# Modulation columns of an MLA layer: twelve more units on TensorE column groups, the last gate's rows moved to the output projection

## The chip, the cores and the metric

The kernel runs on one core of one Trainium2 chip. The metric is device time in microseconds (us) of one execution. Engines are written PE (TensorE), DVE (VectorE), ACT (ScalarE), POOL (GpSimd) and SP (SyncE, whose queue issues the transfers from HBM).

## The reference, cut to what matters

The program computes two blocks, one behind the other, in fp32, on a sequence of 512 tokens and a context of 256, with a width D of 1024. Everything that the change touches lies in the first layer of the first block, an attention layer with low-rank projections (MLA), and in the modulation of that layer and the next:

```python
def modulation(cond, w, bias):
    m = jax.nn.silu(cond) @ w + bias
    return jnp.split(m, 3, axis=-1)

def first_block(x, c, ctx, c_ctx, ada_w, ada_b, norm_g, ...):
    for i in range(DEPTH):                       # DEPTH = 2
        sx, scx, gx = (m[:, None, :] for m in modulation(c, ada_w[i], ada_b[i]))
        sc, scc, gc = modulation(c_ctx, ada_w[i], ada_b[i])
        hx = rms_norm(x, norm_g[i]) * (1 + scx) + sx
        hc = rms_norm(ctx, norm_g[i]) * (1 + scc) + sc
        ...                                      # mixer: h @ w_in, attention, @ w_out
        x = x + gx * yx
        if i < DEPTH - 1:
            ctx = ctx + gc * yc
```

So per layer the vectors `silu(c)` and `silu(c_ctx)` are multiplied with a 1024 x 3072 matrix `ada_w[i]`: shift, scale and gate. The gate of the first layer is needed for both conditions at its output projection, shift and scale of the second layer right behind it, and the gate of the second layer only for `c`, later still.

## The kernel before, in words

Activations lie with the width on the 128 partitions, in eight tiles `k` of 128, and the 768 tokens (256 of context, then 512) along the free dimension. A matrix product in fp32 is made of three PE passes over halves (`mm3`, lines 534 to 538): weights and activations are each split into a rounded high half and the rest (`wh`, `wl`, `hh`, `hl`), and PE multiplies `hh` with `wh`, `hl` with `wh` and `hh` with `wl`. For weights, `wsplit` (from line 511) lets ACT make `wh` (line 519) and DVE make `wl` (line 520); the buffers hold three units, so a unit's split waits until PE has read the unit three before it. `Stream` loads two units by one transfer of 1 MB.

`mla` has three stages. **The input projection** has 14 units of 128 columns. Units 0 to 2 run side by side, over k: for each k, `modulated` (lines 678 to 688) makes `hh` and `hl` from the normed input, with `xr` as the step between (line 686), and then all three units take that k. Units 3 to 13 run one after the other, each over all k, 48 matmuls a unit; ACT evicts units 0 to 4 into `cq`, and units 6 to 13 through Silu into `gate`.

The shift and scale of the first layer come from `modulation(k)`, eight units of 256 columns. Each takes 1 MB of `ada0`, makes eight matmuls of 32 columns (line 776; `sc` holds both conditions in its first columns) that stand in four column groups of the array, copies the result to `mrow` on ACT, sums the four groups and turns the row into columns by two matmuls with the selector `sel` (line 781), and DVE puts them into `md0`. Three places of the tile `ada0` take the loads in turn.

All other modulation columns, 32 tiles of 128, come from `ada_rows`, called after each unit of the projection: 512 KB of the transposed table `adat` go into one of five places, in the still unused ends of `gate` and `cq`, and per row tile and condition one instruction multiplies it with `silu(c)`, spread over all partitions in `crow`, and sums along the free dimension into one column of `mcol`. Most of it is on DVE (line 715). For the second condition two of three row tiles are multiplied on POOL (line 711) and summed on ACT (line 700).

**The attention** of 16 heads stands between, and **the output projection** (`project`, from line 893) has eight units: per unit 24 matmuls for the context and 24 for the sequence, the eviction `L900` on DVE, which multiplies with the gate column of `mcol` and adds to `xc` or `x`, the square on ACT (line 905) and its sum on DVE. The last three units run their context parts first.

The order of each engine's queue is set by a scheduler that goes by the order of the program, with some work lifted ahead (`wsplit` and `wraw` by an offset `WOFF`). The queues are in order, that of SP too: a transfer that waits for its place holds up all behind it.

Of the kernel before, what the change touches and what calls it, by code (L numbers as in the profile page):

```python
# [18 lines left out]
P = 128  # L19
# [76 lines left out]
def layout(inp):  # L96
# [9 lines left out]
    a["crow"] = np.concatenate([f["c"].reshape(1, D), f["c_ctx"].reshape(1, D)], 0)  # L106
# [3 lines left out]
    a["ada0"] = _units(u, KT, 2 * P)  # L110
    rows = np.concatenate([aw[0][:, 2048:].T, aw[1].T], 0).reshape(32, P, D)
    a["adat"] = rows
# [365 lines left out]
class Kern:  # L478
# [211 lines left out]
    def ada_load(self, i):  # L690
        if i < 32:
            self.dma(self.ada_ring[i % len(self.ada_ring)], self.ins["adat"][i])

    def ada_rows(self, n):

        for _ in range(n):
            i = self.ada_i
            if self.ada_pending:
                junk, acc = self.ada_pending.pop()
                self.S.activation(junk, junk, AF.Copy, accum_out=acc)  # L700
            if i >= 32:
                return
            self.ada_i += 1
            w = self.ada_ring[i % len(self.ada_ring)]
            for cond in range(2):
                if cond == 1 and i >= 24:
                    continue
                acc = self.mcol[:, cond, i:i + 1]
                if cond and i % 3:
                    junk = self.apool.tile([P, D], F32, tag="sq", name="junk", bufs=3)  # L710
                    self.G.tensor_tensor(junk, w, self.crow[:, cond], op=ALU.mult)
                    self.ada_pending.append((junk, acc))
                else:
                    junk = self.apool.tile([P, D], BF16, tag="jb", name="junk", bufs=1)
                    self.V.scalar_tensor_tensor(junk, w, 1.0, self.crow[:, cond], op0=ALU.mult, op1=ALU.mult,
                                                accum_out=acc)
            self.ada_load(i + len(self.ada_ring))

    def mla(self):
# [3 lines left out]
        self.ada_i, self.ada_pending = 0, []  # L723
        with ExitStack() as mst:
# [10 lines left out]
            with ExitStack() as st:  # L735
                A = self.apool = self.pool("mlaA", stack=st)
                xt = A.tile([P, KT, TA], F32, tag="xt", name="xt")
                self.crow = A.tile([P, 2, D], F32, name="crow")
# [6 lines left out]
                row = ada0[0:1, 2]  # L745
                self.dma(row, ins["crow"])
# [4 lines left out]
                for k in range(2):  # L751
                    self.dma(ada0[:, k], ins["ada0"][k])
                G.memset(sc, 0.0)
                S.activation(row, row, AF.Silu)
# [4 lines left out]
                for cond in range(2):  # L759
                    G.partition_broadcast(self.crow[:, cond], row[:, cond * D:(cond + 1) * D], channels=P)  # L760
# [3 lines left out]
                def modulation(k):  # L764

                    if k >= KT:
                        return
                    if k >= 2:
                        self.dma(ada0[:, k % 3], ins["ada0"][k])
                    raw = ada0[:, k % 3].rearrange("p (k f) -> p k f", f=2 * P)  # L770
                    md = self.md0[:, k]
# [11 lines left out]
                    V.tensor_scalar(md[:, 0], pm[:, :2], self.vcol("ada_b", k), None, op0=ALU.add)  # L783
                    V.tensor_scalar(md[:, 1], pm[:, 2:], ab1[:, k:k + 1], self.vcol("norm_g", k), op0=ALU.add, op1=ALU.mult)

                acc = self.sumsq(A, [xt[:, k] for k in range(KT)], TA, eng=V, bufs=3)
                self.norm_acc(A, R, acc, TA, D, bufs=3)
                modulation(0)
                win = self.wstream(ins["mw_in"], 14, 2, P)
                fps = [[self.b1(), self.b1()] for _ in range(3)]  # L790
                first = [next(win) for _ in fps]
                modulation(1)
                for k in range(KT):
                    md = self.md0[:, k]
                    self.modulated(A, hh[:, k], hl[:, k], xt[:, k], R, (md[:, 1, 1:2], md[:, 1, 0:1]),
                                   (md[:, 0, 1:2], md[:, 0, 0:1]), segs, "sq", 3)
                    modulation(k + 2)
                    for w, pt in zip(first, fps):
                        for (o, n), ps in zip(segs, pt):
                            self.mm3(ps[:, :n], (w[0][:, k], w[1][:, k]), (hh[:, k, o:o + n], hl[:, k, o:o + n]),  # L800
                                     k == 0, k == KT - 1)
                self.dma(rope, ins["rope"])
                self.woff = WOFF
                cq = A.tile([P, KT, TA], F32, tag="xt", name="cq")
                self.ada_ring = [z[:, o * D:(o + 1) * D] for z, m in (
                    (gate[:, 4:].rearrange("p k t -> p (k t)"), 3), (cq[:, 5:].rearrange("p k t -> p (k t)"), 2))
                    for o in range(m)]
                for i in range(len(self.ada_ring)):
                    self.ada_load(i)
# [896 lines left out]
```

## Time and profile before

| | |
|---|---|
| time of three runs | 1989.47, 1992.1 (median), 1992.36 us |
| profiled execution | 1991.66 us, span of the trace 1989.9 us |
| PE busy | 1874.2 us, 94% of the span |
| DVE busy | 1356.7 us, 68% |
| ACT busy | 948.9 us, 48% |
| POOL busy | 653.9 us, 33% |
| input projection, first to last matmul | 31.4 to 193.4 us of the span |
| output projection, first to last eviction | 499.2 to 557.1 us |

The shares are averages over stages with different limits: PE is busy nearly all the time in most of the program, so what matters for this change is where it is not, in the first 200 us. The times of a row are counted from the start of the span. A busy PE need not be a PE at full clock: the profile lists the granted clock of each stretch.

### The profile page before, as it was taken

The numbers are of one execution on the slowest core, as the hardware profiler recorded it, in microseconds if no ns is written. First come the engines' busy times: TensorE is split into PE (matmuls) and PEld (weight loads), VectorE is DVE, ScalarE is ACT, GpSimd is POOL, SyncE is SP. The second block draws the span as 40 slices with busy tenths as digits, with TensorE's granted clock in tenths as the row PEclk, the third lists the DMA queues.
The fourth block names the chain that finished last, engine by engine and source line by source line (L and its number), as shares of the span: only waits on it lengthen the run. The fifth ranks groups of instructions, "written<-read, shape, count | busy, mean of one in ns | idle before, by whom it ended". The sixth has DMA issues, their size and how long they took to land.

```text
span 1989.9 us, 25452 instructions
## 1 busy us (share of the span) xinstructions
PE 1874.2 (94%) x9842; PEld 1592.4 (80%) x9842; DVE 1356.7 (68%) x1856; ACT 948.9 (48%) x1623; POOL 653.9 (33%) x532
## 2 busy tenths in 40 slices
PE   5888999999989999898889999999999999999997
PEld 3777888898879999787658888888788888888886
DVE  4896777778475556789986666666744466666666
ACT  4463767777264544766535333333422343333333
POOL 0473766755002222555630212121400002121213
PEclk8998999999999999999889999999999999999998
DMA  8543000101121111132112223222222323222221
GB/s 308 184 162 131 27 1 28 43 22 64 53 73 43 44 43 65 49 118 98 48 53 106 106 85 106 88 103 89 96 91 85 106 85 105 86 106 85 106 88 61
DMA packets 33419, 171.28 MB, mean 86 GB/s; under 512 B 3505, under 2 KB 6833, under 8 KB 17809
## 3 DMA queue, kind: packets, MB, share of 16 engines
q1 hardware_dynamic: 33298, 169.65, 24.2%
q8 instruction: 77, 1.26, 0.3%
q14 instruction: 44, 0.36, 0.1%
HBM read 167.54 MB, written 2.10 MB: 85 GB/s over the span
## 4 chain that ended last, share of the span: by engine, by line
PE 46%; DVE 3%; issue 1%; ACT 1%; POOL 0%; DVEq 0%; POOLq 0%; ACTq 0%
PE b L536 15%; PE b L538 15%; PE b L537 15%; DVE cv L1538 0%; DVE x L1657 0%; DVE hl L503 0%; DVE wl L520 0%; DVE hr L1528 0%; DVE x L599 0%; ACT wh L519 0%; PE b L625 0%; DVE yl L499 0%; DVE gt L1275 0%; POOL cv L1569 0%; DVE b L1521 0%
## 5 line engine op out<-in xcount | busy, mean ns | idle before, releaser
L538 PE MATMUL b<-hh,wl 128*128 128x512 f32 (+1 forms) x1248 | 482.8, 388 | 17.1 <-DVE wl L520 17.1
L536 PE MATMUL b<-hh,wh 128*128 128x512 f32 (+1 forms) x1248 | 485.4, 392 | 9.5 <-ACT hh L687 5.1
L537 PE MATMUL b<-hl,wh 128*128 128x512 f32 (+1 forms) x1248 | 482.6, 387 | 3.6 <-DVE hl L503 3.6
L519 ACT CAST wh<-raw 128x1024 fp32r<-128x1024 f32 (+1 forms) x257 | 263.5, 1026 | 462.5 <-PE b L537 416.1
L538 PEld LDWEIGHTS b<-hh,wl 128*128 128x128 f32 x1248 | 239.2, 192 | 68.2 <-DVE wl L520 17.9
L520 POOL TENSOR_TENSOR wl<-raw,wh 128x1024 fp32r<-128x1024 f32 (+1 forms) x68 | 166.2, 2446 | 381.1 <-ACT wh L519 374.4
L520 DVE TENSOR_TENSOR wl<-raw,wh 128x1024 fp32r<-128x1024 f32 (+1 forms) x189 | 246.8, 1308 | 60.6 <-ACT wh L519 56.6
L536 PEld LDWEIGHTS b<-hh,wh 128*128 128x128 f32 x1248 | 238.2, 191 | 58.8 <-ACT hh L687 6.1
L537 PEld LDWEIGHTS b<-hl,wh 128*128 128x128 f32 x1248 | 239.3, 192 | 56.3 <-DVE hl L503 4.9
L1538 DVE SCALAR_TENSOR_TENSOR cv<-u,vec,cv 128x511 f32<-128x511 f32 x192 | 181.0, 943 | 41.3 <-ACT cv L1536 39.3
L1564 DVE TENSOR_TENSOR u<-b,Rp 128x512 f32<-128x512 f32 x88 | 60.8, 691 | 157.5 <-PE b L538 157.0
L1569 POOL TENSOR_TENSOR cv<-cv 128x512 f32<-128x512 f32 x44 | 57.2, 1300 | 267.8 <-DVE cv L1538 211.6
L536 PE MATMUL b<-ah,wh 128*128 128x512 f32 (+1 forms) x368 | 140.1, 382 | 0.0
L538 PE MATMUL b<-ah,wl 128*128 128x512 f32 (+1 forms) x368 | 140.0, 381 | 0.0
L537 PE MATMUL b<-al,wh 128*128 128x512 f32 (+1 forms) x368 | 139.8, 380 | 0.0
L1589 DVE TENSOR_TENSOR x<-x,b 128x512 f32<-128x512 f32 x160 | 105.3, 679 | 11.3 <-PE b L538 11.0
L536 PE MATMUL b<-wh,hh 128*128 128x256 f32 (+1 forms) x320 | 95.7, 301 | 2.6 <-ACT wh L519 2.6
L1536 ACT ACTIVATE cv<-u,vec 128x512 f32<-128x512 f32 x96 | 78.2, 814 | 35.7 <-DVE u L1564 35.7
L537 PE MATMUL b<-wl,hh 128*128 128x256 f32 (+1 forms) x320 | 93.8, 293 | 0.0
L1024 DVE TENSOR_REDUCE st<-b 128x1 f32<-128x768 f32 (+1 forms) x96 | 74.0, 772 | 28.9 <-PE b L538 28.1
L538 PE MATMUL b<-wh,hl 128*128 128x256 f32 (+1 forms) x320 | 93.1, 293 | 0.0
L1029 POOL TENSOR_SCALAR p<-p,st 128x768 f32<-128x768 f32 (+1 forms) x96 | 73.5, 768 | 56.2 <-DVE st L1028 49.5
(399 smaller groups left out, 3997.8 us busy)
## 6 DMA issues: line engine op xcount, KB each, us to landing
raw<-in_fw_up SPq DMA_DIRECT2D x44, 1024.0 KB, 4.8
raw<-in_fw_dn SPq DMA_DIRECT2D x22, 1024.0 KB, 4.8
raw<-in_ow_in SPq DMA_DIRECT2D x12, 1024.0 KB, 4.8
gate<-in_adat SPq DMA_DIRECT2D x20, 512.0 KB, 4.5
ada<-in_ada SPq DMA_DIRECT2D x8, 1024.0 KB, 7.6
raw<-in_mw_in SPq DMA_DIRECT2D x7, 1024.0 KB, 6.3
cq<-in_adat SPq DMA_DIRECT2D x12, 512.0 KB, 3.5
raw<-in_mw_out SPq DMA_DIRECT2D x4, 1024.0 KB, 4.9
```

Of the source, the lines that this page charges most:

```text
L519: self.S.copy(hi, raw[:, o:o + w])
L520: (leng or self.V).tensor_tensor(lo, raw[:, o:o + w], hi.bitcast(F32), op=ALU.subtract)
L536: m(out, w[0], x[0], start=start, stop=False)
L537: m(out, w[0], x[1], start=False, stop=False)
L538: m(out, w[1], x[0], start=False, stop=stop)
L1024: V.tensor_reduce(st[:, 0:1], sv, axis=AX.XY, op=ALU.max, negate=True)
L1029: G.tensor_scalar(p[:, :nk * P], p[:, :nk * P], st[:, 2:3], 0.0, op0=ALU.mult, op1=ALU.add)
L1536: self.S.activation(v, u, AF.Identity, bias=col(3), scale=col(2))
L1538: self.V.scalar_tensor_tensor(v[:, sh:], u[:, :T - sh], col(tap), v[:, sh:], op0=ALU.mult, op1=ALU.add)
L1564: V.tensor_tensor(u, ps, R, op=ALU.mult)
L1569: G.tensor_tensor(cv[0], cv[0], cv[1], op=ALU.mult)
L1589: V.tensor_tensor(self.x[:, 4 * j + f], self.x[:, 4 * j + f], ps, op=ALU.add)
```

## The change

The 24 row tiles that hold the first layer's gate and the second layer's shift and scale are taken from DVE and POOL and become twelve more units of 256 columns, of the kind of `modulation(k)`, which is now split into `ada_load`, `ada` (the load's use: eight matmuls and the copy to `mrow`) and `columns` (the selector matmuls and what DVE makes of them). Units 8 and 9 stand behind units 0 to 2 of the projection, then one stands behind each unit up to the twelfth; the selector matmuls of each come a unit later, ahead of its k = 6. Their loads go into a ring of three places of 1 MB: a tile `spare`, the end of `cq` and the end of `gate`. The eight row tiles of the second layer's gate stay on DVE, for `c` alone, in the output projection (`gate1`), with a buffer `g1` of one place and with `crow` loaded there. At the start of the program the squares of the odd tiles are summed by PE and those of the even ones by DVE. `silu` on one partition and the two broadcasts on POOL go.

```diff
     a["crow"] = f["c"].reshape(1, D)
...
-    def ada_rows(self, n):
-
-        for _ in range(n):
-            i = self.ada_i
-            if self.ada_pending:
-                junk, acc = self.ada_pending.pop()
-                self.S.activation(junk, junk, AF.Copy, accum_out=acc)
...
-                if cond and i % 3:
-                    junk = self.apool.tile([P, D], F32, tag="sq", name="junk", bufs=3)
-                    self.G.tensor_tensor(junk, w, self.crow[:, cond], op=ALU.mult)
-                    self.ada_pending.append((junk, acc))
-                else:
-                    junk = self.apool.tile([P, D], BF16, tag="jb", name="junk", bufs=1)
-                    self.V.scalar_tensor_tensor(junk, w, 1.0, self.crow[:, cond], op0=ALU.mult, op1=ALU.mult,
-                                                accum_out=acc)
-            self.ada_load(i + len(self.ada_ring))
...
+                def ada(i):
+
+                    raw = slots[i].rearrange("p (k f) -> p k f", f=2 * P)
 
                     pr = self.b1()[:, :2 * P]
                     for kk in range(KT):
                         j = 32 * (kk % 4)
                         PE.matmul(pr[j:j + 32], sc[:, kk], raw[:, kk], start=(kk < 4), stop=(kk >= 4))
-                    mrow = A.tile([P, 2 * P], F32, tag="mrow", name="mrow", bufs=1)
+                    mrow = A.tile([P, 2 * P], F32, tag="mrow", name="mrow", bufs=2)
                     S.copy(mrow, pr)
+                    return i, mrow
+
+                def columns(i, mrow):
+
                     pm = self.b1()[:, :4]
                     for part in range(2):
                         PE.matmul(pm[:, 2 * part:2 * part + 2], mrow[:, part * P:(part + 1) * P], sel,
                                   start=True, stop=True)
...
+                    c = 2 * (i - KT)
+                    V.tensor_copy(self.mcol[:, :, c:c + 2], pm.rearrange("p (k c) -> p c k", c=2))
...
-                acc = self.sumsq(A, [xt[:, k] for k in range(KT)], TA, eng=V, bufs=3)
+                for k in range(KT):
+                    q = acc if k == 0 else A.tile([P, TA], F32, tag="sq", name="sq", bufs=3)
+                    i = S.activation(q, xt[:, k], AF.Square)
+                    if k % 2:
+                        for (o, e), ps in zip(segs0, pss):
+                            PE.matmul(ps[:, :e - o], self.ones, q[:, o:e], start=k == 1, stop=False)
+                    elif k:
+                        V.tensor_tensor(acc, acc, q, op=ALU.add)
...
+                ring = [spare, cq[:, 5:].rearrange("p k t -> p (k t)")[:, :2048],
+                        gate[:, 5:].rearrange("p k t -> p (k t)")[:, :2048]]
+                last = 20
+                for i in range(KT, last):
+                    slots[i] = ring[(i - KT) % 3 if i < 19 else 0]
+                for i in range(KT, KT + 3):
+                    ada_load(i)
+                rest = iter(range(KT, last))
+                rows = []
...
                     for k in range(KT if u >= len(fps) else 0):
+                        if k == 6 and rows:
+                            columns(*rows.pop())
                         for (o, n), ps in zip(segs, pt):
...
-                    self.ada_rows(3 if u < 3 else 4)
+                    for i in ((next(rest, None),) if u > 1 else ()):
+                        if i is not None:
+                            rows.append(ada(i))
+                            if i + 3 < 19:
+                                ada_load(i + 3)
...
+                def gate1(f):
+                    w = C.tile([P, D], F32, tag="g1", name="g1", bufs=1)
+                    self.dma(w, ins["adat"][f])
+                    V.scalar_tensor_tensor(w, w, 1.0, crow, op0=ALU.mult, op1=ALU.mult, accum_out=gsum[:, f:f + 1])
...
                     project(f, w, 0)
+                    gate1(f)
...
                 self.lastx = project(7, w[2], 0)
+                for f in range(5, KT):
+                    gate1(f)
+                V.tensor_tensor(self.mcol[:, 0, 24:], gsum, self.vcol("ada_b", 40, 8), op=ALU.add)
```

The order of DVE between the units 5 and 8 of the projection, before. Rows `L715` are the reductions of `ada_rows`, rows `L520` the weight splits, `L818` the norm of `cq`:

```order
L520 TENSOR_TENSOR wl<-raw,wh 128x1024
L715 SCALAR_TENSOR_TENSOR junk,mcol<-gate,crow 128x1024
L499 TENSOR_TENSOR krs<-kr,krs 32x768
L715 SCALAR_TENSOR_TENSOR junk,mcol<-cq,crow 128x1024 x3
L715 SCALAR_TENSOR_TENSOR junk,mcol<-gate,crow 128x1024
L818 SCALAR_TENSOR_TENSOR cq<-cq,vec,R_916 128x768 x2
L715 SCALAR_TENSOR_TENSOR junk,mcol<-gate,crow 128x1024
L520 TENSOR_TENSOR wl<-raw,wh 128x1024
```

and of the change (`L519` is now the split, `L758` the copy of two columns into `mcol`):

```order
L519 TENSOR_TENSOR wl<-raw,wh 128x1024
L498 TENSOR_TENSOR krs<-kr,krs 32x768
L758 COPY mcol<-b_858 128x2x2
L519 TENSOR_TENSOR wl<-raw,wh 128x1024
L818 SCALAR_TENSOR_TENSOR cq<-cq,vec,R_876 128x768 x2
```

Between two splits six reductions are gone, and a small copy has come, which takes its input from PE.

The order of PE where units 0 to 2 of the projection end and unit 3 begins, of the change (`L749` are selector matmuls, `L740` the 32-column matmuls, of unit 9 here):

```order
L537 MATMUL b_164<-hh,wl 128x512
L749 MATMUL b_548<-sel,mrow 128x2 x2
L740 MATMUL b_552<-cq,sc 32x256 x8
L535 MATMUL b_564<-hh,wh 128x256
L536 MATMUL b_564<-hl,wh 128x256
```

Before, the matmuls of unit 3 stood there at once. Now the selector of modulation unit 8 and all of unit 9 stand ahead of them.

The order of DVE in the output projection, the change, from unit 3's eviction to the split of unit 7 (`L913` is `gate1`, `L922` the eviction, `L928` the sum of squares, `L519` the split):

```order
L922 SCALAR_TENSOR_TENSOR x<-b_5514,mcol,x 128x512
L913 SCALAR_TENSOR_TENSOR g_5841,gsum<-g_5841,crow 128x1024
L519 TENSOR_TENSOR wl<-raw,wh 128x1024
L928 TENSOR_TENSOR accx<-accx,q 128x512
L922 SCALAR_TENSOR_TENSOR xc<-b_5552,mcol,xc 128x256
L913 SCALAR_TENSOR_TENSOR g_5844,gsum<-g_5844,crow 128x1024
L928 TENSOR_TENSOR accc<-accc,q 128x256
L922 SCALAR_TENSOR_TENSOR x<-b_5581,mcol,x 128x512
L913 SCALAR_TENSOR_TENSOR g_5847,gsum<-g_5847,crow 128x1024
L519 TENSOR_TENSOR wl<-raw,wh 128x1024
```

Before, the same rows stood there without `L913`. All eight of its rows now stand ahead of the last split, the last three of them ahead of the splits of units 6 and 7.

## Rows read from the trace of the kernel before

**Rows 1.** Windows, core 0: stretch, length, busy us (instructions) per engine, PEclk, DMA share, GB/s

```profile
62.00:75.00 13.00, 7.68 (x28) 5.74 (x26) 12.65 (x19) 5.45 (x11) 6.72 (x3) 0.74 0.56 201
125.00:160.00 35.00, 21.84 (x104) 18.90 (x105) 34.77 (x27) 23.89 (x34) 24.95 (x9) 0.75 0.41 139
```

**Rows 2.** Waits of PE, 30 to 200 us: us in total, times, longest

```profile
PE b L538 <- DVE wl L520: 17.1, 3, 10.6
PE b L536 <- ACT hh L687: 5.1, 2, 2.8
```

**Rows 3.** Timeline of PE: start us, us, engine, line, op, out<-in, [idle before <-releaser]

```profile
31.36 0.56 PE L536 MATMUL b<-hh,wh 128*128 128x256 f32 x1
...
63.46 0.39 PE L538 MATMUL b<-hh,wl 128*128 128x512 f32 x1
...
66.63 0.62 PE L536 MATMUL b<-hh,wh 128*128 128x256 f32 x3 [2.78 <-ACT hh L687]
...
74.98 0.39 PE L536 MATMUL b<-hh,wh 128*128 128x256 f32 x1 [0.19 <-ACT wh L519]
...
127.55 0.58 PE L538 MATMUL b<-hh,wl 128*128 128x256 f32 x1 [5.57 <-DVE wl L520]
...
157.38 0.58 PE L538 MATMUL b<-hh,wl 128*128 128x256 f32 x1 [10.62 <-DVE wl L520]
...
158.19 0.63 PE L537 MATMUL b<-hl,wh 128*128 128x512 f32 x1
...
193.40 0.28 PE L536 MATMUL b<-cqh,wh 128*128 128x256 f32 x1
```

**Rows 4.** Tile junk: instructions, ns min/median/max, first and last start

```profile
L715 DVE SCALAR_TENSOR_TENSOR junk<-gate,crow x25: 1211/1225/3423, 60.9 to 175.2; 128x1024 bf16<-128x1024 f32 x25
...
L711 POOL TENSOR_TENSOR junk<-gate,crow x10: 2482/3107/3394, 62.7 to 145.9; 128x1024 f32<-128x1024 f32 x10
```

**Rows 5.** Timeline of DVE: two weight splits, beside POOL and alone

```profile
154.51 2.82 DVE L520 TENSOR_TENSOR wl<-raw,wh 128x1024 fp32r<-128x1024 f32 x1
...
163.91 1.22 DVE L520 TENSOR_TENSOR wl<-raw,wh 128x1024 fp32r<-128x1024 f32 x1
```

**Rows 6.** Timeline of PE: modulation units of two k steps, and a sum of squares

```profile
46.44 0.50 PE L781 MATMUL b<-sel,mrow 128*128 128x2 f32 x4
...
46.87 1.07 PE L776 MATMUL b<-ada,sc 128*32 128x256 f32 x16
...
51.11 0.50 PE L781 MATMUL b<-sel,mrow 128*128 128x2 f32 x4
...
93.80 1.45 PE L591 MATMUL b<-sqa,ones 128*128 128x512 f32 x4
```

**Rows 7.** Timeline of ACT: evictions of two units without halts

```profile
184.51 0.39 ACT L847 ACTIVATE gate<-b 128x256 f32<-128x256 f32 x1 [6.55 <-PE b L538]
...
192.91 0.39 ACT L847 ACTIVATE gate<-b 128x256 f32<-128x256 f32 x1 [6.34 <-PE b L538]
```

**Rows 8.** Timeline of PE: the start of the program

```profile
18.02 2.90 PE L591 MATMUL b<-sqa,ones 128*128 128x512 f32 x4 [18.02 <-DVE sqa L578]
...
26.53 1.93 PE L776 MATMUL b<-ada,sc 128*32 128x256 f32 x16 [0.16 <-DMA ada<-in_ada]
...
30.49 1.01 PE L781 MATMUL b<-sel,mrow 128*128 128x2 f32 x4 [2.03 <-ACT mrow L778]
```

**Rows 9.** Timeline of DVE: evictions and the last weight split of the output projection

```profile
501.06 0.75 DVE L900 SCALAR_TENSOR_TENSOR x<-b,mcol,x 128x512 f32<-128x512 f32 x1 [1.37 <-PE b L538]
...
532.49 1.23 DVE L520 TENSOR_TENSOR wl<-raw,wh 128x1024 fp32r<-128x1024 f32 x1
...
537.39 0.48 DVE L900 SCALAR_TENSOR_TENSOR xc<-b,mcol,xc 128x256 f32<-128x256 f32 x1 [1.42 <-PE b L538]
```

**Rows 10.** Page, part 6: issues, KB each, median us from issue to landing

```profile
gate<-in_adat SPq DMA_DIRECT2D x20, 512.0 KB, 4.5
...
cq<-in_adat SPq DMA_DIRECT2D x12, 512.0 KB, 3.5
```

More of the change, by code (lines that the diff above doesn't have):

```diff
@@ L109, in layout @@
     u = aw[0][:, :2 * D].reshape(D, 2, KT, P).transpose(0, 2, 1, 3).reshape(D, 2 * D)
-    a["ada0"] = _units(u, KT, 2 * P)
-    rows = np.concatenate([aw[0][:, 2048:].T, aw[1].T], 0).reshape(32, P, D)
-    a["adat"] = rows
+    a["ada"] = _units(np.concatenate([u, aw[0][:, 2 * D:], aw[1][:, :2 * D]], 1), KT, 2 * P)
+    a["adat"] = np.ascontiguousarray(aw[1][:, 2 * D:].T).reshape(KT, P, D)
+    a["crow"] = f["c"].reshape(1, D)
     w = f["mla_w_in"][0]
@@ L744, in mla @@
                 sel = A.tile([P, 2], F32, name="sel")
-                row = ada0[0:1, 2]
-                self.dma(row, ins["crow"])
+                spare = A.tile([P, 2048], F32, name="spare")
                 self.dma(self.vec, ins["vec"])
@@ L750, in mla @@
                     self.dma(xt[:, k], ins["xt"][:, k * TA:(k + 1) * TA])
-                for k in range(2):
-                    self.dma(ada0[:, k], ins["ada0"][k])
+                self.dma(ada0[:, 0], ins["ada"][0])
                 G.memset(sc, 0.0)
-                S.activation(row, row, AF.Silu)
                 S.activation(sc[:, :, :2].rearrange("p k c -> p c k"),
@@ L758, in mla, with ada_load @@
                 V.tensor_reduce(sel, self.ident.rearrange("p (j c) -> p c j", j=4)[:, :2], axis=AX.X, op=ALU.add)
-                for cond in range(2):
-                    G.partition_broadcast(self.crow[:, cond], row[:, cond * D:(cond + 1) * D], channels=P)
                 ab1 = A.tile([P, KT], F32, name="ab1")
                 V.tensor_scalar(ab1, self.vcol("ada_b", 8, 8), 1.0, None, op0=ALU.add)
[L764 to L771, printed above, removed]
+                slots = {k: ada0[:, k % 3] for k in range(KT)}
+                def ada_load(i):
+                    self.dma(slots[i], ins["ada"][i])
+                def ada(i):
+                    raw = slots[i].rearrange("p (k f) -> p k f", f=2 * P)
                     pr = self.b1()[:, :2 * P]
@@ L789, in mla @@
+                self.table = self.ln_exp_table(i)
+                for (o, e), ps in zip(segs0, pss):
+                    PE.matmul(ps[:, :e - o], self.ones, acc[:, o:e], start=False, stop=True)
+                    tmp = A.tile([P, TA], F32, tag="sq", name="rt", bufs=3)[:, :e - o]
+                    self.rstd(R[:, o:e], ps[:, :e - o], D, tmp, self.table)
                 win = self.wstream(ins["mw_in"], 14, 2, P)
                 fps = [[self.b1(), self.b1()] for _ in range(3)]
-                first = [next(win) for _ in fps]
@@ L792, in mla @@
-                modulation(1)
+                first = [next(win)]
+                ada_load(1)
+                columns(*ada(0))
+                first += [next(win), next(win)]
+                ada_load(2)
+                columns(*ada(1))
                 for k in range(KT):
@@ L796, in mla @@
                                    (md[:, 0, 1:2], md[:, 0, 0:1]), segs, "sq", 3)
[L797 to L800, printed above, removed]
+                    if k + 3 < KT:
+                        ada_load(k + 3)
+                    rows = ada(k + 2) if k + 2 < KT else None
+                    for n, (w, pt) in enumerate(zip(first, fps)):
+                        for (o, m), ps in zip(segs, pt):
+                            self.mm3(ps[:, :m], (w[0][:, k], w[1][:, k]), (hh[:, k, o:o + m], hl[:, k, o:o + m]),
                                      k == 0, k == KT - 1)
+                        if n == 0 and rows:
+                            columns(*rows)
                 self.dma(rope, ins["rope"])
@@ L856, in mla @@
                         self.split(krh, krl, kr[64:96])
-                    self.ada_rows(3 if u < 3 else 4)
+                    for i in ((next(rest, None),) if u > 1 else ()):
[3 more added lines that the diff above has]
+                                ada_load(i + 3)
+                            elif i == 17:
+                                ada_load(19)
+                            if u == 2:
+                                columns(*rows.pop())
+                                rows.append(ada(next(rest)))
+                                ada_load(i + 4)
             self.psum(4)
```

40 lines of the change are left out of this document (15 added, 25 removed).

## The prediction, made before the changed kernel had run

> **What bounds the kernel now.** I read the windows view over the first 200 us first. TensorE (PE) is idle 13.2 of the 35 us from 125 to 160 and 5.3 of the 13 us from 62 to 75, and its granted clock averages 0.75 and 0.74 of full speed there, while VectorE (DVE) is busy all through [rows 1]. The waits of PE name the cause: 17.1 us for `wl`, the low halves of the projection's weights, which DVE makes, and 5.1 us for `hh`, whose input `xr` DVE makes [rows 2]. The timeline shows the places: 2.78 us before 66.63, 5.57 us before 127.55, 10.62 us before 157.38 [rows 3]. After a long halt PE runs at the lower level of its clock (1.2 GHz): a 512-wide matmul takes 0.63 us at 158.19, 0.39 us at 63.46 [rows 3].
>
> DVE is late because of the rows of the table `adat`. It makes 40 reductions of them (32 rows, and every third of the 24 that serve both conditions again), with a median of 1.225 us but up to 3.42 us for the 25 that come from `gate`, and GpSimd (POOL) multiplies the other 16 at about 3.1 us each [rows 4]. A weight split of 1.22 us takes 2.82 us while POOL computes [rows 5]: the two engines slow each other. The Trainium skill ("GPSIMD Engine Reference", Specifications) says that POOL shares VectorE's SBUF interfaces and collides with DVE instructions that read two SBUF inputs; by that rule these rows must shrink once POOL's products are gone, and the trace agrees (1.22 against 2.82 us).
>
> **The change, part by part.** The sum is made against the profiled execution, 1991.66 us (span 1989.9 and 1.8 around it), 0.4 us below the median of 1992.1. A measurement tells about 0.2%, 4 us, from no change.
>
> *What the halts cost.* One unit of 48 matmuls takes 8.40 us at full clock (the evictions at 184.51 and 192.91 [rows 7]), so the 18 matmuls of one k step over three units take 3.15. From the first projection matmul at 31.36 to the first of attention at 193.40 [rows 3] are 162.0 us. Needed are 14 units of 8.40, 117.6; five modulation units; and two sums of squares of 1.45 [rows 6], 2.9. A modulation unit (eight 32-column matmuls and two selector matmuls) costs 1.52: one k step with it takes 4.67 us (46.44 to 51.11 [rows 6]), without it 3.15. Five are 7.6, the sum is 128.1, and 33.9 us are lost. By place: from 31.36 to the matmul at 63.46 and 0.23 us on stand 32.3 us for seven k steps and the five units (29.6), so 2.7 are lost, to the lower clock; from there to the first matmul of the fourth unit at 74.98 stand 11.3 us for one k step, 8.1 lost to halts and clock; the last 118.4 us hold eleven units and the two sums (95.3), 23.1 lost.
>
> *What is removed.* The 40 DVE reductions and 16 POOL products between 60 and 178 us, the sums on ScalarE (ACT) behind the latter, and their 32 loads. DVE keeps per 10 us unit one split of 1.22 us and a few small operations, and in the order as it is now each split stands ahead of, or only behind, work that does not wait on a load. I take the halts on `wl` and `hh` as gone and with them their clock loss. Left of the 33.9 I keep 4.2: the 2.7 of the cold start and 1.5 for new waits, above all unit 9, whose load goes into `cq`, memory of `xt`, and so is issued only behind the last `xr`. The ends are 1 and 12 us (a halt like the one at 127.55 with its clock loss remains).
>
> *What is added on PE.* Twelve modulation units, and one more selector pair falls behind the first projection matmul: 12 times 1.52 plus 0.43 (46.44 to 46.87 [rows 6]), 18.7 us, all on PE, which sets the end here. The Trainium skill ("TensorEngine Tiling (Array Packing)", Key Properties) speaks against this: changing the tiling mode drains TensorE, so that each unit would pay twice on top of its matmuls. The price of 1.52 was taken as the difference of two periods and holds such drains; the busy times alone are 1.07 and 0.50 [rows 6], so no drain beyond them shows. The selector matmuls wait for `mrow` from ACT; put at k = 6 of the next unit they have 6 us of matmuls ahead of them. The loads of the units (1 MB each, a ring of three places) are issued nearly three units of 9.9 us ahead.
>
> *The start.* The squares of odd tiles go to PE as five pairs of matmuls instead of one. A pair takes 2.90 us cold [rows 8]; the first four run while `xt` still arrives, and at the clock's upper level, which they may win, each is 1.45. In the order PE then needs units 0, 1 and 2 before the first projection matmul. The third unit's load bound PE at 26.53 [rows 8] and is still the fifth megabyte behind `xt`; but the selector of unit 2, which waited for ACT until 30.49, no longer stands ahead. So the first matmul comes at about 28, and one more microsecond goes for k = 1. Against 31.36 I take 2.3 us gained; ends 0 and 4.
>
> *The output projection.* DVE gets eight reductions (1.225 and 0.08 for reading the sum, 1.30). PE alone bounds this stage, and DVE's queue is in order. `g1` has one buffer: each load waits for the reduction before it, and behind the reduction stands the next weight split. The last split, of unit 7, now ends at 533.7 (532.49 and 1.23) and PE wants it from about 537.6, just behind the eviction at 537.39 [rows 9]. The chain from the eviction at 501.06 on [rows 9] is eight reductions (10.4), seven loads and the split (1.2). At 3.5 us per load (`cq<-in_adat` [rows 10]) it ends at 537.2; two of the loads share the queue with others, for which I add 2.0: 539.2, a halt of 1.6, taken as 2.0 with its wake. At 4.5 (`gate<-in_adat` [rows 10]) it is 7 more, 9.0. Lower end 0. Silu of `crow` on ACT stands ahead of a weight cast that PE wants two units later.
>
> *The sum:* 1991.66 - 2.3 - 33.9 + 4.2 + 18.7 + 2.0 = 1980.4 us. Attention and all behind the output projection stay as they are.
>
> **The rivals.**
> *A, the forecast:* the DVE halts go, PE pays for the units: about 1978 to 1985.
> *B, all goes well:* clock up at the start, 1 us of new waits, no halt in the output projection: 1991.66 - 4 - 33.9 + 18.7 + 1, about 1973.5. For it speaks that loads are issued far ahead; against it that the first matmul still waits for 5 MB.
> *C, the chain of `g1` grows:* at 4.5 us per load the halt is 9.0 and the time 1987.4. It decides at 5.1 us per load: there the halt, 2.0 and seven times 1.6, equals the 13.3 us won elsewhere. At 7 us the halt is 26.5 and the time 2005, **slower than before**. For it: one buffer, and a median of 4.5 in the `gate` row. Against: that median is of loads among others, and here the queue is nearly empty.
> *D, the large halt stays:* the split behind 146 us is held not by DVE but by ACT, whose order around unit 6 and 7 switches tables between Silu and the norm, and evicts late. Then 10.6 us and some 2.5 of clock remain, and with 18.7 us more on PE the time is about 1993.5, no change. Against it: the split began at 154.51 [rows 5], with DVE busy throughout [rows 1] on reductions ahead of it in its order.
>
> **How the numbers follow.** A 0.58, B 0.15, C up to 1988 0.11, C beyond break-even 0.05, D 0.08, anything else (a late unit load, say) 0.03. The predicted time is A's, 1980.4. The range 1973 to 1990 takes in A, B and the mild C, and leaves D and the strong C out. Faster by over 0.2% is below 1988.1: A, B and most of mild C, 0.84. Slower, above 1996.1: 0.06. The rest, 0.10.
>
> **What would show it.** Right: PE's waits for `wl` from 30 to 200 us fall from 17.1 to under 3; the first attention matmul comes at about 180 instead of 193.4; a unit's period between modulation units is near 9.9 us; the splits on DVE return to 1.22. In the output projection a wait of PE for `wl` of up to 3 us stands before the unit 7 matmuls. Wrong: a wait of PE for a load of `ada` units or for `mrow` of several us per unit; a period well over 9.9, which would make the 1.52 too low; reductions in the output projection that wait over 4 us each; or attention that starts no sooner than 188.

## The result and the profile after

The changed kernel takes 1978.01 us (median of 4 runs, 1977.14 to 1978.75) against 1992.23 us (4 runs) before: ratio 0.9933, 95% interval 0.9921 to 0.9945. The forecast was 1980.4 in 1973 to 1990, so the time and the sign were right. The profiled execution has a span of 1975.6 us, 14.3 less than before. PE is busy 1887.0 us (96%), DVE 1272.2 (64%), ACT 932.0 (47%), POOL 591.6 (30%).

The windows of the stretches that showed the halts [rows 1]:

```profile
62.00:75.00 13.00, 13.00 (x93) 10.68 (x86) 5.83 (x7) 9.46 (x15) 0.00 (x0) 1.00 0.88 335
125.00:160.00 35.00, 35.00 (x241) 28.26 (x244) 4.33 (x7) 7.71 (x15) 0.00 (x0) 1.00 0.27 99
```

PE (first pair after the width) is busy throughout at full clock, DVE (third) falls to 4.33 of 35 us, POOL is at rest. The waits of PE from 20 to 200 us, where `wl` stood with 17.1 and `hh` with 5.1 [rows 2], are now all of them:

```profile
PE b L740 <- DMA ada<-in_ada: 3.8, 1, 3.8
PE b L749 <- ACT mrow L742: 0.5, 1, 0.5
PE b L535 <- ACT hh L686: 0.2, 1, 0.2
PE b L535 <- DVE v L990: 0.2, 1, 0.2
```

The only large one is in the start, for the load of modulation unit 1. The timeline of PE, with the line numbers of the changed kernel (L535 to L537 the three matmuls of a product, L740 a unit, L749 its selector):

```profile
17.15 1.07 PE L740 MATMUL b<-ada,sc 128*32 128x256 f32 x16
...
23.38 1.93 PE L740 MATMUL b<-ada,sc 128*32 128x256 f32 x16 [3.76 <-DMA ada<-in_ada]
...
28.62 0.58 PE L535 MATMUL b<-hh,wh 128*128 128x256 f32 x1
...
66.40 1.07 PE L740 MATMUL b<-cq,sc 128*32 128x256 f32 x16
...
119.16 1.07 PE L740 MATMUL b<-spare,sc 128*32 128x256 f32 x16
126.57 0.50 PE L749 MATMUL b<-sel,mrow 128*128 128x2 f32 x4
129.21 1.07 PE L740 MATMUL b<-cq,sc 128*32 128x256 f32 x16
...
179.35 0.33 PE L535 MATMUL b<-cqh,wh 128*128 128x256 f32 x1
```

The first projection matmul comes at 28.62 (before 31.36), the first of attention at 179.35 (before 193.40, [rows 3]). A period from one unit to the next is 10.05 us. Of the new units none stands with a wait. The eleven weight splits of the stretch took up to 3.42 us before (first line, with ns min/median/max). They take 1.22 to 1.29 now, and it is they that wait, for ACT's cast; before, DVE never sat idle ahead of one:

```profile
L520 DVE TENSOR_TENSOR wl<-raw,wh x11: 1212/1219/3419, 75.0 to 176.8; 128x1024 fp32r<-128x1024 f32 x11
...
L519 DVE TENSOR_TENSOR wl<-raw,wh x11: 1224/1226/1290, 66.1 to 150.3; 128x1024 fp32r<-128x1024 f32 x11
its engine sat idle before it (us, times) until:
  ACT wh L518: 19.1, 7
```

In the output projection the timeline of DVE shows the chain of `g1` (L913 reductions) and the last split (L519):

```profile
486.15 0.48 DVE L922 SCALAR_TENSOR_TENSOR xc<-b,mcol,xc 128x256 f32<-128x256 f32 x1 [2.59 <-PE b L537]
487.48 1.22 DVE L913 SCALAR_TENSOR_TENSOR g<-g,crow 128x1024 f32<-128x1024 f32 x1 [0.84 <-DMA g<-in_adat]
488.63 0.75 DVE L922 SCALAR_TENSOR_TENSOR x<-b,mcol,x 128x512 f32<-128x512 f32 x1
...
521.89 1.23 DVE L913 SCALAR_TENSOR_TENSOR g<-g,crow 128x1024 f32<-128x1024 f32 x1 [2.56 <-DMA g<-in_adat]
...
523.04 1.22 DVE L519 TENSOR_TENSOR wl<-raw,wh 128x1024 fp32r<-128x1024 f32 x1
524.86 0.48 DVE L922 SCALAR_TENSOR_TENSOR xc<-b,mcol,xc 128x256 f32<-128x256 f32 x1
```

From the first reduction to the last are seven steps, 34.4 us, 4.9 each. The split ends at 524.3, just ahead of the eviction before unit 7, and PE does not wait for it.

### The profile page after: what moved, and what is told of

It is laid out like the page before. It is cut to its first block, busy times and chain, and to the rows that moved or that the text cites. A ratio compares the mean times of both kernels' runs of the same rounds, so it can differ in the third digit from the quotient of the medians.

```text
span 1975.6 us, 25804 instructions
## 1 busy us (share of the span) xinstructions
PE 1887.0 (96%) x10098; PEld 1599.0 (81%) x10098; DVE 1272.2 (64%) x1801; ACT 932.0 (47%) x1601; POOL 591.6 (30%) x514
## 3 DMA queue, kind: packets, MB, share of 16 engines
q8 instruction: 79, 1.29, 0.3%
## 4 chain that ended last, share of the span: by engine, by line
PE 46%; DVE 4%; issue 1%; ACT 1%; POOL 0%; DVEq 0%; POOLq 0%; ACTq 0%
PE b L535 15%; PE b L537 15%; PE b L536 15%; DVE cv L1564 0%; DVE x L1683 0%; DVE hl L502 0%; DVE wl L519 0%; DVE hr L1554 0%; DVE x L598 0%; ACT wh L518 0%; PE b L624 0%; DVE yl L498 0%; DVE gt L1301 0%; POOL cv L1595 0%; DVE b L1547 0%
## 5 line engine op out<-in xcount | busy, mean ns | idle before, releaser
L535 PE MATMUL b<-hh,wh 128*128 128x512 f32 (+1 forms) x1248 | 482.2, 389 | 4.0 <-DVE uu L1305 2.7
L536 PE MATMUL b<-hl,wh 128*128 128x512 f32 (+1 forms) x1248 | 477.6, 383 | 3.7 <-DVE hl L502 3.7
L537 PE MATMUL b<-hh,wl 128*128 128x512 f32 (+1 forms) x1248 | 477.6, 383 | 0.0
L519 DVE TENSOR_TENSOR wl<-raw,wh 128x1024 fp32r<-128x1024 f32 (+1 forms) x189 | 239.9, 1272 | 86.1 <-ACT wh L518 76.7
L519 POOL TENSOR_TENSOR wl<-raw,wh 128x1024 fp32r<-128x1024 f32 (+1 forms) x68 | 166.2, 2446 | 418.6 <-ACT wh L518 418.4
L535 PEld LDWEIGHTS b<-hh,wh 128*128 128x128 f32 x1248 | 235.3, 189 | 56.7 <-issue 7.7
L537 PEld LDWEIGHTS b<-hh,wl 128*128 128x128 f32 x1248 | 235.6, 189 | 49.5 <-issue 0.4
L535 PE MATMUL b<-ah,wh 128*128 128x512 f32 (+1 forms) x368 | 140.1, 382 | 0.0
L537 PE MATMUL b<-ah,wl 128*128 128x512 f32 (+1 forms) x368 | 140.0, 381 | 0.0
L535 PE MATMUL b<-wh,hh 128*128 128x256 f32 (+1 forms) x320 | 96.2, 303 | 2.6 <-ACT wh L518 2.6
L537 PE MATMUL b<-wh,hl 128*128 128x256 f32 (+1 forms) x320 | 93.0, 292 | 0.0
```

Of the source, the lines that this page charges most:

```text
L519: (leng or self.V).tensor_tensor(lo, raw[:, o:o + w], hi.bitcast(F32), op=ALU.subtract)
L535: m(out, w[0], x[0], start=start, stop=False)
L536: m(out, w[0], x[1], start=False, stop=False)
L537: m(out, w[1], x[0], start=False, stop=stop)
```

## The experiments

All ratios are to runs of the kernel before on the same chip. The theory: in the kernel before DVE was late because it and POOL worked on `adat` at once and slowed each other; with both engines off that work PE runs through, and pays for the twelve units in full. The rivals: the order of DVE's queue alone (a split behind reductions that wait for loads), POOL or ACT alone, or a price of the units that is hidden.

**e1 and e2: one half of the work on `adat` at a time.** In the kernel before, in `ada_rows`:

```
e1:
                 if cond and i % 3:
-                    self.G.tensor_tensor(junk, w, self.crow[:, cond], op=ALU.mult)
-                    self.ada_pending.append((junk, acc))
+                    continue
e2:
                 else:
-                    self.V.scalar_tensor_tensor(junk, w, 1.0, self.crow[:, cond], op0=ALU.mult, op1=ALU.mult,
-                                                accum_out=acc)
+                    pass
```

Both also set `mcol` to zero at the start, so that the sums that are left out are zero.

> The kernel before with the 16 products on POOL and the 16 sums of them on ACT left out (those sums then stay zero); the 40 reductions on DVE and all 32 loads stay. Theory (DVE is late because it and POOL slow each other; the reductions alone would fit): DVE has at most 5.3 reductions of 1.225 us and one split of 1.22 us in a unit of 8.4 us, so the waits of PE for wl fall from 17.1 to under 4 us and most of the 33.9 us come back: 1964 us, between 1958 and 1970. Rival (the order of DVE's queue: a split stands behind reductions that wait for their loads, with POOL or without): at least half of the loss stays, 1975 us or more, and the reductions of the gate rows wait on DMA.

> The kernel before with the 40 reductions on DVE left out (those sums stay zero); POOL's 16 products, ACT's 16 sums and all 32 loads stay. Theory: the splits that meet a product of POOL still take 2.8 us, but DVE has little else, so no split is late: waits for wl under 2 us, time 1961 us (1957 to 1966). Rival (POOL's products alone hold DVE up enough, or ACT's sums do): waits for wl of 5 us or more, time above 1970.

e1: 1965.87 us, ratio 0.9876 (0.9859 to 0.9893). e2: 1961.55 us, 0.9856 (0.9841 to 0.9871). Both lie in the range of the theory. For e1, the wait of PE for `wl`, and the groups by tile (count, then ns min/median/max) of DVE's reductions of `gate` rows and of its splits:

```profile
PE b L538 <- DVE wl L520: 1.6, 1, 1.6
...
L714 DVE SCALAR_TENSOR_TENSOR junk<-gate,crow x25: 1217/1224/2171, 60.0 to 146.6; 128x1024 bf16<-128x1024 f32 x25
...
L520 DVE TENSOR_TENSOR wl<-raw,wh x11: 1215/1222/1325, 70.6 to 148.2; 128x1024 fp32r<-128x1024 f32 x11
```

and for e2 the same wait, POOL's products of `gate` rows and DVE's splits:

```profile
PE b L538 <- DVE wl L520: 0.3, 1, 0.3
...
L712 POOL TENSOR_TENSOR junk<-gate,crow x10: 2390/2411/3473, 62.2 to 123.1; 128x1024 f32<-128x1024 f32 x10
...
L520 DVE TENSOR_TENSOR wl<-raw,wh x11: 1224/1226/3433, 67.6 to 139.1; 128x1024 fp32r<-128x1024 f32 x11
```

With all 40 reductions there, e1's waits of PE for `wl` are 1.6 us instead of 17.1. With POOL's 16 products and ACT's 16 sums all there, e2's are 0.3, though a split beside POOL still takes up to 3.43: POOL or ACT alone does not make the halts. In e1 ACT's sums go too, so that DVE's reductions with ACT's sums and without POOL's products were not run. DVE's order is made anew for each program and is not quite the same in e1: at most five reductions stand between two splits, before it was six. That the reductions waited for their loads is ruled out by the kernel before itself, where DVE has almost no idle time from 75 to 160 us:

```profile
75.00:160.00 85.00, 67.43 (x354) 57.28 (x355) 84.50 (x66) 54.59 (x81) 61.30 (x22) 0.90 0.48 165
```

What filled its queue is seen in the timelines of DVE and POOL. Between 70 and 160 us 14 of its reductions and splits took 2.27 to 3.43 us instead of 1.22, 26.6 us more in all. All 14 began while POOL was in an operation, nine (19.0 of the 26.6 us) while it was in a product and five, the 2.82 us split of [rows 5] among them, while it was in other work (the split of `cql`, the step on `kr`). In e1, with no product and no sum on ACT, five reductions still took 2.17 to 2.87 us, some 7 us more in all, each beside that other work of POOL. So what lengthens DVE's operations is POOL, for the most part by its products. Each of the 14, and of the five, ends 1.08 or 1.09 us behind the end of the POOL operation that ran when it began. One such pair in the kernel before:

```profile
137.34 2.99 POOL L711 TENSOR_TENSOR junk<-gate,crow 128x1024 f32<-128x1024 f32 x1 [1.50 <-DMA gate<-in_adat]
137.99 3.42 DVE L715 SCALAR_TENSOR_TENSOR junk<-gate,crow 128x1024 bf16<-128x1024 f32 x1
```

POOL ends at 140.33, DVE at 141.41: the operation that begins second seems to stand until the first has ended. Six reductions and splits that began up to 0.5 us ahead of a product took 1.21 to 1.22. One reduction of e1 does not fit: it began at 98.28, inside an operation of POOL that lasted from 97.45 to 101.21, and took 1.22. The Trainium skill ("GPSIMD Engine Reference", Specifications) says that POOL shares VectorE's SBUF interfaces; these rows agree, and POOL's products too are quicker without DVE's reductions (those of `gate` rows: 2.41 us in the median, 3.11 before, [rows 4]).

**e3: all 56 reductions on DVE.** The same place, `if False:` for `if cond and i % 3:`.

> The kernel before with POOL's 16 products and ACT's sums made on DVE as reductions like the other 40, nothing left out. Theory: 48 of the 56 reductions stand in the first seven units, 59 us at 1.225 us besides some 25 us of splits and norms, where PE needs about 55 us; so DVE is again the bound there, and only the last seven units are free of halts: 1970 to 1985 us. Rival (only POOL's presence makes DVE late, its number of reductions doesn't): 1964 us or less. The reductions all take about 1.23 us in both, none over 1.5.

1969.63 us, 0.9896 (0.9881 to 0.991): the computation is whole and faster than the change, though DVE has 16 reductions more than before. The time lies just below the range, and the place did not come as expected: no wait for `wl` remains, the splits take 1.22 to 1.32, and DVE catches up behind them, with 14 reductions behind the last split and 34.24 us busy of 35 from 125 to 160. That no reduction would take over 1.5 us was wrong too: seven took 2.17 to 3.29, beside POOL's other work. What is late is the eviction of `gate`, whose memory the last rows still hold, ahead of the first matmul of attention:

```profile
167.21 0.39 PE L536 MATMUL b<-cqh,wh 128*128 128x256 f32 x1 [3.14 <-ACT gate L845]
```

**e4: the change with the 24 rows on DVE instead of the units.** Two rows of two reductions in each of units 2 to 13, a ring of five places, and `crow` for both conditions made at the start again as before. Cut to the calls, the last line in short:

```
-                    rows.append(ada(i))
+                    for _ in range(2 if u > 1 else 0):
+                        row_sum(next(rest))      # two V.scalar_tensor_tensor, both conditions
```

> The changed kernel with its twelve modulation units taken off PE again: the 24 rows of adat that they stand for go to DVE as 48 reductions, two rows (four reductions) in each of the units 2 to 13, none on POOL; start and output projection as in the change. Theory: 4.9 us of reductions, 1.22 of split and about 1 of the rest fit into a unit of 8.4 us, so PE gets back the 12 units (12 times 1.55 to 1.65 us) and loses at most 3 us to late splits: 1961 us, between 1956 and 1968, faster than the change. Rival (any reductions ahead of a split in DVE's order bring the halts back): 1975 us or more, with PE waiting for wl 5 us or more.

1962.14 us, 0.986 (0.9845 to 0.9875). As the theory had it; the interval of the change's ratio lies wholly above it. From the windows:

```profile
75.00:100.00 25.00, 25.00 (x141) 21.50 (x140) 23.79 (x31) 12.20 (x18) 9.41 (x5) 1.00 0.58 202
100.00:125.00 25.00, 25.00 (x142) 21.55 (x141) 22.83 (x26) 15.32 (x20) 8.55 (x4) 1.00 0.17 64
125.00:160.00 35.00, 35.00 (x201) 30.59 (x201) 27.36 (x42) 7.51 (x12) 1.90 (x2) 1.00 0.54 174
160.00:195.00 35.00, 31.55 (x186) 28.43 (x185) 25.54 (x40) 23.60 (x47) 25.02 (x22) 0.93 0.18 61
```

DVE is busy 23.79 and 22.83 of 25 us and 27.36 of 35, 87% of the time from 75 to 160 (95% in e3), and PE does not stand once there in either. So a DVE that is busy nearly all through need not hold PE up; before it had next to no idle time (84.50 of 85 us), and its splits came late. At the start of attention PE stands 3.45 of 35 us here.

**e5: the change without its units.** `rows.append(ada(i))` taken out, and what hangs on it; the loads stay.

> The changed kernel without its twelve modulation units in the projection (their eight matmuls each, the copy of mrow and the selector matmuls are left out, so that mcol stays zero for the first three parts); their twelve loads of 1 MB stay. Theory (the units lie wholly on PE's path, at the period seen in the change, 10.05 us less 8.40): 12 times 1.65 is 19.8 us less than the change, 1958 us; at the 1.52 of the prediction it would be 1960. Rival (part of each unit fills time in which PE would wait anyway): less than 15 us, 1963 or more, with waits of PE for wl or hh of 4 us or more in the trace.

1961.23 us, 0.985 (0.9836 to 0.9863), between the two expectations. The first matmul of the projection and of attention:

```profile
28.27 0.58 PE L535 MATMUL b<-hh,wh 128*128 128x256 f32 x1
...
159.88 0.28 PE L535 MATMUL b<-cqh,wh 128*128 128x256 f32 x1
```

In the traces the stretch between them is 150.73 us in the change and 131.61 here: 19.1 us for twelve units, 1.59 each. Of them 1.1 come back in attention (297.9 us from its first matmul to that of the output projection, 296.8 in the change) and 0.2 in the output projection (68.1 us from its first matmul to its last eviction, 67.9 in the change). At the start of attention PE now waits 1.6 us each for `qh` and `ql`, which it did not in the change, and its clock drops:

```profile
160.00:195.00 35.00, 31.53 (x185) 28.72 (x184) 20.46 (x35) 24.81 (x49) 22.07 (x18) 0.90 0.12 38
```

**e6: the selector at once.** `columns(*ada(i))` in the place of `rows.append(ada(i))`, the call at `k == 6` removed.

> The changed kernel with each unit's selector matmuls straight behind its eight matmuls instead of at k = 6 of the next unit (eleven units differ). Theory: PE stands each time for ACT's copy of mrow, at least the 0.49 us seen in the start, up to 1.4 us where ACT is in an eviction: 5 to 15 us in all, 1988 us (1983 to 1994), and the row of waits for mrow grows from 1.3 us to 6 or more. Rival (the wait is hidden, since the next unit's matmuls need a fresh accumulator anyway): under 2 us, 1978 to 1980.

2000.63 us, 1.0048 (1.0035 to 1.0062): slower than before, above the range, and 22.6 us above the change where 5 to 15 were expected. From 64 to 200 us PE's waits read

```profile
PE b L749 <- ACT mrow L742: 15.4, 11, 3.7
```

Eight of the eleven are 0.5 to 0.7 us, three 3.0 to 3.7. One of the longest, 3.67 us at unit 6, is explained by the rows of ACT ahead of its copy (L742):

```profile
121.50 1.28 ACT L563 ACT_TABLE_LOAD   x1
122.79 1.05 ACT L563 ACTIVATE rt<-b,eps 128x512 f32<-128x512 f32 x2
123.86 1.28 ACT L566 ACT_TABLE_LOAD   x1
125.16 0.63 ACT L566 ACTIVATE R<-rt 128x512 f32<-128x512 f32 x1
125.69 0.35 ACT L742 COPY mrow<-b 128x256 f32<-128x256 f32 x1
```

So the mechanism held. The mean of 1.4 us a wait is the upper end that was expected, but by three long waits behind a chain on ACT, and not because each was that long. From the first projection matmul to the first of attention are 172.03 us (29.14 to 201.17), 21.3 more than in the change. Of these 15.4 are the waits; for the other 5.9 PE is busy longer with the same work (156.4 against 150.5), at a lower granted clock behind the long waits, which I had left out. The first of the windows:

```profile
62.00:75.00 13.00, 9.98 (x64) 7.94 (x57) 5.73 (x7) 9.46 (x15) 0.00 (x0) 0.77 0.89 341
```

**e7: the old sum of squares in the start.** `sumsq` and `norm_acc` as in the kernel before, all else changed.

> The changed kernel with the sum of squares at the start as before: DVE adds all seven tiles, and one pair of matmuls per segment follows. Theory: unit 0 comes 1 to 2 us later and PE enters it at the lower clock; the first projection matmul at about 30 instead of 28.6: 1979.5 us (1978.5 to 1981.5). Rival (the start waits for the load of unit 1, whatever the sums do): first matmul within 0.3 us of 28.6 and no difference, 1978.

1982.77 us, 0.9958 (0.9944 to 0.9971), above the range. The first projection matmul comes at 30.14, 1.5 later, as expected. The profile's span is 4.2 longer, though: 1.4 more is a wait for `wl` in the output projection. The last split stands behind the last reduction as in the change, but it begins 38.5 us behind the first `xc` eviction (487.31 to 525.81), in the change 36.9 (486.15 to 523.04). The rows of DVE, and the wait of PE (us in total, times, longest):

```profile
487.31 0.48 DVE L908 SCALAR_TENSOR_TENSOR xc<-b,mcol,xc 128x256 f32<-128x256 f32 x1 [2.59 <-PE b L537]
...
524.66 1.23 DVE L899 SCALAR_TENSOR_TENSOR g<-g,crow 128x1024 f32<-128x1024 f32 x1 [2.67 <-DMA g<-in_adat]
...
525.81 1.22 DVE L519 TENSOR_TENSOR wl<-raw,wh 128x1024 fp32r<-128x1024 f32 x1
...
PE b L537 <- DVE wl L519: 1.4, 1, 1.4
```

The halt forecast for the change exists, then, and sets in where the split begins about 37 us behind that eviction; the change only just escapes it. The other 1.3 us of the 4.2 lie behind the output projection, where the two kernels are alike.

**e8 and e10: two refinements of e4.** e8 moves `ada_load(1)` ahead of `first = [next(win)]`, and unit 2 behind two thirds of the first k step. e10 ends the rows a unit sooner and puts the small sums on `mcol` on DVE.

> The version with the 24 rows spread on DVE, and in the start the load of modulation unit 1 ahead of the second weight load; unit 2 then comes on PE behind two thirds of the first k step. Theory: the 3.7 us for which PE waits for unit 1's load shrink by about 2.5 us, the time of one load of 1 MB, and the clock stays up: 1959.6 us (1957.5 to 1961). Rival (the start is bound by the bytes of all its loads, so the wait moves to wl of the second weight load): 1962 us within 1.

> The version with the rows on DVE and the early load of unit 1, with the rows ended one unit sooner (three rows in each of units 11 and 12, none in 13; the places in gate used until their tile is evicted), and the small sums and copies on mcol on DVE instead of POOL, where they held up the weight splits of attention. Theory: the casts of kh on DVE and the splits on POOL at the start of attention come 3 to 4 us sooner, and of the 3 us of waits for qh and ql and the lower clock (0.95) between 160 and 195 us about 2.5 go: 1958.8 us (1956.5 to 1960.5). Rival (those waits come from PE's own evictions and the chain q, rope, qh on ACT and POOL, whatever DVE does): no difference, 1961 us within 1.

e8: 1961.32 us, 0.9851 (0.9838 to 0.9865), just above the theory's range and within the rival's. e10, which is e8 with two more edits: 1959.58 us, 0.9839 (0.9823 to 0.9854), in its range. In e8 the wait for unit 1's load falls from 3.7 to 1.2 us and the first projection matmul comes at 24.29 instead of 29.38, but attention only 2.2 earlier (160.06 against 162.28). In e10 the waits for `qh` and `ql`, most of which were to go, are 1.6 and 1.4 (in e8 1.6 and 1.5), so its time was met by luck. The intervals of e4, e8 and e10 overlap: neither step is shown to gain. All three beat both kernels, by about 1.5% and 0.8%.

**e9: the chain of `g1` made long.** One line more in `gate1`:

```
+                    self.dma(w, ins["adat"][(f + 1) % KT])
                     self.dma(w, ins["adat"][f])
```

> The changed kernel with two loads of 512 KB into g1 ahead of each of the eight reductions of the last gate, the second behind the first. In the change a step of that chain takes 4.8 us, and the split of unit 7 ends 36.9 us behind the first eviction of the output projection, at about the point from which PE waits. Theory (rival C of the prediction is real, the change only just keeps clear of it): a step takes about 8 us, the last split comes some 22 us later, PE waits for wl in the output projection by 18 to 26 us in all, with some clock lost: 2000 us (1995 to 2006), slower than before. Rival (the splits can go ahead of the reductions, or other work fills the time): under 5 us, 1978 to 1983.

1989.01 us, 0.9985 (0.9976 to 0.9994): 11 us above the change, half of what the theory asked, more than the rival allowed, and not slower than before. A step takes some 8.5 us as expected, but the scheduler put DVE's operations in another order: the last split (519.62) now stands ahead of four of the reductions. PE waits for `wl` no more than in the change; what is held up is what stands behind the reductions, the next stage's input from `xc`. The rows of DVE:

```profile
519.62 1.23 DVE L519 TENSOR_TENSOR wl<-raw,wh 128x1024 fp32r<-128x1024 f32 x1
525.69 1.22 DVE L914 SCALAR_TENSOR_TENSOR g<-g,crow 128x1024 f32<-128x1024 f32 x1 [4.24 <-DMA g<-in_adat]
...
551.08 1.23 DVE L914 SCALAR_TENSOR_TENSOR g<-g,crow 128x1024 f32<-128x1024 f32 x1 [1.94 <-DMA g<-in_adat]
```

and of PE, with the waits that follow:

```profile
547.49 0.34 PE L256 MATMUL b<-hch,wr 128*64 128x256 f32 x1 [3.31 <-ACT hch L686]
553.42 0.42 PE L257 MATMUL b<-hcl,wr 128*32 128x256 f32 x1 [3.29 <-DVE hcl L687]
```

## Why the prediction was right, by its steps

| step | forecast | measured in the two profiles |
|---|---|---|
| start | -2.3 | -2.7 (31.36 to 28.62) |
| halts and clock of the input projection gone | -33.9 | -33.9, with what is left over: |
| left over there | +4.2 | +3.1 (150.73 less 128.1 needed less 19.5) |
| twelve units and the selector pair on PE | +18.7 | +19.5 (19.1 of e5, which keeps the pair, and 0.43) |
| output projection | +2.0 | 0.0 (first to last eviction 57.9 us in both) |
| the rest, to the end | 0 | -0.3 (attention 1.0 longer, behind the output projection 1.3 shorter) |

- **The start.** The gain was near the forecast, its reason only in part. Of the 2.7 us 1.5 come with the new sums of squares (e7). The prediction had PE bound by the load of the third modulation unit, which rests on a wait of 0.16 us [rows 8]; in the change PE stands 3.76 us for the load of the second, and its clock falls.
- **What is removed.** Right, and e1 and e2 show the reason given for it: reductions and products together make DVE late, either half alone does not. One row of the argument was misread: the split of 2.82 us [rows 5] stood beside POOL's split of `cql`, not beside a product. The change keeps that work of POOL; its one weight split that meets POOL takes 1.29 us. The signs named for this stage came: no wait for `wl`, splits at 1.22, attention at 179.35 where about 180 was said, a period of 10.05 for 9.9. The wait for `wl` before unit 7 in the output projection did not come. Rival D is out: the 10.6 us are gone, though ACT's loads of tables around unit 6 are still there:

```profile
109.28 1.28 ACT L563 ACT_TABLE_LOAD   x1
...
111.64 1.28 ACT L566 ACT_TABLE_LOAD   x1
```

- **What is left over.** Unit 9, for whose load into `cq` I had kept most of 1.5 us, did not wait. Some 3.0 of the 3.1 lie ahead of unit 9's first matmul at 66.40: from 28.62 to there are 37.8 us, of which 34.8 are needed (three units of 8.40, five modulation units of 1.52, a selector pair of 0.43, one unit of 1.59). They begin at the lower clock: PE has stood 3.76 us for unit 1's load (L740 takes 1.07 us at 17.15, 1.93 at 23.38), and a 256-wide matmul takes 0.58 at 28.62, 0.33 at 179.35. The granted clock is 0.51 from 28.6 to 32.4 us and 1.00 from 32.4 to 36, which makes some 1.9 of the 3.0 by my estimate; the rest is not placed.
- **What is added on PE.** 1.59 per unit for 1.52. The period of 10.05 less 8.40 gives 1.65, and PE does not stand in it; e5's 1.59 is a little low, since PE is idle 1.08 us in e5's stretch and 0.23 in the change's. The busy times, 1.07 and 0.50, come to 1.57. The Trainium skill ("TensorEngine Tiling (Array Packing)", Key Properties) says that a change of the tiling mode drains TensorE; beyond the busy times a unit costs at most 0.08 us here. That the selector must wait a unit was right, and worth 22.6 us (e6), more than the whole gain.
- **The output projection.** This is the term that was mis-sized, by its 2.0 us. The mechanism was right: I let the chain begin behind the eviction, and added 2.0 for loads that share the queue. It began 1.2 us ahead of that eviction (487.48 against 488.63), and with the split it took 36.8 us where 38.1 were reckoned. The loads took the 3.5 us that the sum had for them (median of the eight transfers into `g1` in the change, from issue to landing). The point from which PE waits was right to within half a microsecond (e7).
- **Rival C.** At loads of 3.5 us it did not arise. Its price is not tested by e9: with a step of 8.5 us, 7.2 a load, it would give over 2000 us, and e9 took 1989, but in another order of DVE, where the halts land on the next stage. What slower loads would cost in the change's own order, and so the break-even of 5.1 us per load, stays open. In that order e7 alone bears on it: the split began 1.6 us later against the eviction, and PE waited 1.4.

The span fell by 14.3 us where 11.3 were forecast. Of the 3.0 between, 2.0 are the output projection, 0.4 the start and 0.3 the rest; what is left over, 1.1 less than forecast, and the units, 0.8 more, make the last 0.3. The time behind the output projection differs by up to 3 us between profiles of kernels that are alike there (1431.5 in the change, 1432.8 before, 1434.6 in e3), so the last microsecond can't be placed.

## What to carry to other kernels

A helper engine that slows the one it relieves can cost more than it takes over: price both engines' operations from rows in which both run, look where each long one ends, and try first to keep all the work on one of them and spread it evenly (e3 was one line). Work moved to the engine that bounds a stage is paid in full, here 19.1 us to get rid of 33.9, so look at once for an idle engine in the same stage; in the changed kernel DVE was idle for 30 of 35 us, and e4 took the units back there. A value that passes from PE over ACT to PE again is put a unit apart, since the waits cost the clock as well (e6).

## What was not expected of the hardware

- Waits cost more than their length: in e6 eleven waits of 15.4 us in sum made the input projection 21.3 us longer, with the granted clock at 0.77 from 62 to 75 us, where it was 1.00 in the change. Behind the first of the three long ones, 3.02 us, it was 0.50 for 4.5 us (70.5 to 75).
- DVE and POOL do not slow each other by a share: all 14 long reductions and splits of the kernel before began inside an operation of POOL and end 1.08 or 1.09 us behind its end, and those that began just ahead of a product took 1.21 to 1.22. POOL's product of a `gate` row has a median of 2.41 us where DVE has only splits (e2), 3.11 before [rows 4].
- PE's clock fell in the start after one wait of 3.76 us: the granted clock was 1.00 from 16 to 19.6 us, 0.50 (the lower level, 1.2 GHz) from 23.4 to 28.6 and 0.51 on to 32.4, and the same sixteen instructions of a unit took 1.07 us before the wait and 1.93 after it.
